# A hybrid decoder layer in split fp32: the sample columns of both FFNs' gate/up moved into the combined products

## The chip, the cores and the metric

The kernel runs on one core of a Trainium2 chip. The metric is the device time of one execution in microseconds; times are medians of several runs on the same chip. One execution was profiled.

## What is computed

One layer for 1024 prompt tokens and 64 sample tokens (8 sequences of 8) that share the weights. `D_MODEL` is 1024, `D_FF` 2816.

```python
def swiglu(x, w_gu, w_down):
    g, u = jnp.split(x @ w_gu, 2, axis=-1)
    return (jax.nn.silu(g) * u) @ w_down

# run_layer, per token group
x = x + 0.5 * rms_norm(swiglu(rms_norm(x, norm_ffn1_pre), ffn1_w_gu, ffn1_w_down), norm_ffn1_post)
h = rms_norm(x, norm_mix_pre)
z = h @ w_in + b_in            # q, k, v of the attention; q, f, i, g of the recurrence
a = rms_norm(windowed_attention(q, k, v, sinks), attn_out_norm)
o = rms_norm(hgrn2(hq, hf, hi), hg_out_norm) * silu(hg)
x = x + rms_norm(concat(a, o) @ w_out, norm_mix_post)
x = x + 0.5 * rms_norm(swiglu(rms_norm(x, norm_ffn2_pre), ffn2_w_gu, ffn2_w_down), norm_ffn2_post)
```

Outputs are the new activations of both groups, the key and value windows and the recurrent states.

## The kernel before

**Split products.** Every large fp32 product is made of three matmuls on rounded halves: an operand is split into `hi` (a copy rounded to fp32r, on ScalarE, line 240) and `lo` (the difference, on VectorE, line 241), and `mm3` (lines 258 to 262) accumulates hi x hi, hi x lo and lo x hi in one PSUM bank. L260, L261 and L262 in the profile are these three. In names, `wsph`/`wspl` are the halves of a weight tile of a head unit, `w` those of a combined product's weights, `h` those of activations, `mm` a PSUM bank.

**Chunks.** The tokens are cut into three chunks: chunk 0 has 256 prompt and the 64 sample tokens (320 columns), chunks 1 and 2 have 384 prompt tokens each.

**Gate/up.** Chunk 0's gate and up are direct products. One head unit `j` (`up0`, line 730; 22 units an FFN) has a g and a u bank, 8 steps of k in each and three matmuls a step, 48 matmuls of 320 columns. `gated0` (line 712) evicts them: in the first FFN both banks are multiplied by `rb` (the root of the pre-norm, lines 718 and 725), Silu runs on ScalarE, and g times u is line 726; in the second FFN the input is normed already and rb is absent. Chunks 1 and 2 are made together by a fast matrix scheme: seven products a unit, 22 units an FFN, each product 4 steps of three matmuls of 384 columns, on seven operands `SF[1..7]` that `pre_x` (first FFN) or `pre_s` with `sums_s` (second) and `factor` prepare. `begin`, `prepare`, `product`, `evict` and `left` make the steps of `up`. In the first FFN `HEAD1 = 9` puts 18 of the 22 chunk-0 units ahead, and the other four are made inside `up` as pieces (`piece`, line 860).

**Order of the work.** The kernel is one stream of program text; a scheduler of the tile framework sets the order of each engine. Beside the large products run "streams": generators that `tick()` (line 102) advances at a given rate, and that `need(name)` runs to their end. `p1` prepares the operands in the first FFN's head. The mixer of each chunk (`m0`, `m1`, `m2`: attention and recurrence) and the norms (`c0`, `c1`, `c2`) run beside the projections and beside the second FFN's head units, which are dealt out by `HEAD2 = (4, 13, 22)`: 4 units, then w_out of chunk 1, then units 4 to 13 beside `m2`, then w_out of chunk 2, then the last 8 beside `c2`. In the mixer, `sc` are attention scores, `pT` the transposed probabilities (TensorE, line 1269, copied by VectorE at 1274), `pv` their product with the values (line 1283).

Weights are loaded by SP's queue; three raw buffers, and `loads0` keeps up to three tiles prepared ahead.

Of the kernel before, what the change touches and what calls it, by code (L numbers as in the profile page):

```python
# [25 lines left out]
WIDTH = [320, 384, 384]  # L26
BLK0 = [0, 2, 5]
# [20 lines left out]
def tile_step(ctx: ExitStack, tc: tile.TileContext, A: dict, O: list):  # L48
# [20 lines left out]
    def hslot(n):  # L69
        w = WIDTH[n]  # L70
        return pp.tile([P, 4, w], F32R, tag=f"h{w}", bufs=8 if w == 384 else 4, name=uid("h"))

    def big(dt=F32, shape=(P, 4, 384)):
        return pp.tile(list(shape), dt, tag="big", bufs=12, name=uid("big"))
# [36 lines left out]

    def need(name):
        st = streams.pop(name, None)
        if st is not None:
            for _ in st[0]:
                pass
# [6 lines left out]
    ones = cp.tile([P, P], F32, name="ones")  # L123
    V.memset(ones, 1.0)
    junk = cp.tile([P, 512], BF16, name="junk")
    omean = cp.tile([P, P], F32, name="omean")
    V.memset(omean, 1.0 / D)
    S.activation(junk[:, :P], ones, AF.Silu)
    cols = cp.tile([P, NROWS], F32, name="cols")
    f1pre = cp.tile([P, KC], F32, name="f1pre")  # L130
    halfpost = cp.tile([P, 16], F32, name="halfpost")
    nsinkb = cp.tile([P, 8], F32, name="nsinkb")
    amask = cp.tile([P, 192], F32, name="amask")
    amask1 = cp.tile([P, P], F32, name="amask1")
    smask = cp.tile([P, 136], F32, name="smask")
    ssink = cp.tile([P, 2], F32, name="ssink")
    seqm = cp.tile([P, 4], F32, name="seqm")
    lmask = {h: cp.tile([P, 32], U8, name=f"lm{h}") for h in LEVELS[2:]}
    ident32 = cp.tile([P, 32], F32, name="ident32")
# [3 lines left out]
    def gains():  # L143
        nc.sync.dma_start(cols, A["cols"])
        V.tensor_scalar(halfpost[:, 0:8], cols[:, C_F1POST:C_F1POST + 8], 0.5, None, op0=ALU.mult)
        V.tensor_scalar(halfpost[:, 8:16], cols[:, C_F2POST:C_F2POST + 8], 0.5, None, op0=ALU.mult)

    def mix_consts():
# [4 lines left out]
        band = tmp2("band", (P, 256))  # L153
        V.memset(band, 0.0)
        G.affine_select(band, band, pattern=[[1, 256]], compare_op=ALU.is_ge, fill=NEG,
                        base=0, channel_multiplier=-1)
        G.affine_select(band, band, pattern=[[-1, 256]], compare_op=ALU.is_ge, fill=NEG,
                        base=P, channel_multiplier=1)
        V.tensor_copy(amask[0:64], band[0:64, 0:192])
        V.tensor_copy(amask[64:P], band[64:P, 64:256])  # L160
        V.tensor_copy(amask1, amask[:, 64:192])
        V.memset(amask1[0:64, 0:64], NEG)
# [5 lines left out]

        s5 = tmp[:, 3, 0:32]
        V.tensor_scalar(s5, row[:, 0:32], 31, None, op0=ALU.bitwise_and)  # L170
        V.tensor_tensor(x[:, 0:32], col[:, 0:32], s5, op=ALU.bitwise_xor)
        V.tensor_copy(tf[:, 1, 0:32], s5)
        V.tensor_copy(tf[:, 1, 32:64], col[:, 0:32])
        V.tensor_tensor(tf[:, 0, 0:32], tf[:, 1, 32:64], tf[:, 1, 0:32], op=ALU.is_gt)
        V.tensor_tensor(ident32, tf[:, 1, 32:64], tf[:, 1, 0:32], op=ALU.is_equal)
        for i, h in enumerate(LEVELS[2:]):
            V.tensor_scalar(tmp[:, 3, 32:64], x[:, 0:32], 4 - i, None, op0=ALU.logical_shift_right)
            V.tensor_copy(tf[:, 1, 64:96], tmp[:, 3, 32:64])
            V.scalar_tensor_tensor(lmask[h], tf[:, 1, 64:96], 1.0, tf[:, 0, 0:32],
                                   op0=ALU.is_equal, op1=ALU.mult)  # L180
# [16 lines left out]
        V.tensor_tensor(smask, tf2[:, 2], tf2[:, 3], op=ALU.add)  # L197

        e = cp.tile([P, 3, 4], F32, name="lbe")
# [34 lines left out]
    def small():  # L234
        return pp.tile([P, 4, 8], F32, tag="small", bufs=10, name=uid("sm"))
# [51 lines left out]
    def tmp2(name, shape=(P, 512)):  # L287
# [1627 lines left out]
```

## Time and profile before

| | |
|---|---|
| median of 3 runs | 1937.2 us (1936.32 to 1937.89) |
| profiled execution: its span, which is its whole time | 1937.4 us |
| TensorE matmuls | 1923.1 us, 13547 |
| VectorE | 1430.7 us, 2469 |
| ScalarE | 946.0 us, 1701 |
| GpSimd | 186.1 us, 227 |
| DMA | 375.56 MB, mean 194 GB/s |

The stages, read from the timeline's changes of matmul shape: first FFN's head 5.65 to 137.8 us; its combined products to 480.5; down and the mixer's first parts to 1106; four head units of the second FFN to 1135; w_out of chunk 1 to 1179.6; ten head units beside `m2` to 1282; w_out of chunk 2 to 1315.2; eight head units beside `c2` to 1374.1; combined products of the second FFN to 1689; down to the end.

A row of the timeline has start, duration, engine, line, operation, output and inputs, shape. A row of the groups has busy time and mean duration behind the first bar and the idle time before them, with what ended it, behind the second. PE is TensorE's matmuls, PEld its weight loads, DVE VectorE, ACT ScalarE, POOL GpSimd, SP SyncE.

### The profile page before, as it was taken

Reading aid. Unit: us, or ns where it says so; the run is one execution under the profiler, and the core shown is the slowest. Engines: PE = TensorE matmul, PEld = TensorE weight load, DVE = VectorE, ACT = ScalarE, POOL = GpSimd, SP = SyncE. Lnnn points to the kernel's source line nnn. Section 1 sums busy time; section 2 is a strip of 40 time slices with the busy share of each in tenths; the row PEclk is TensorE's granted clock in tenths of the full one; section 3 lists DMA queues with packets and bytes.
Section 4 is the critical chain, followed back from the end, with each engine's and each line's share of the span. In section 5 each row is a group of like instructions: output and inputs, shape, how many; then the busy total and the mean of one; then the engine's idle time right before and its main releaser. Section 6 shows DMA issues by size and latency. Waiting matters only on the chain.

```text
span 1937.4 us, 34843 instructions
## 1 busy us (share of the span) xinstructions
PE 1923.1 (99%) x13547; PEld 1806.1 (93%) x13547; DVE 1430.7 (74%) x2469; ACT 946.0 (49%) x1701; POOL 186.1 (10%) x227
## 2 busy tenths in 40 slices
PE   9999999999999999999999999999999999999998
PEld 9999999999998987788999888989999999999886
DVE  6896789877568666787678758756987887656666
ACT  5553444444455434545445545846544444445452
POOL 0300000000004022020221212000000000000102
PEclk9999999999999999999999999999999999999999
DMA  6643676555767556765334344546555555667974
GB/s 248 209 133 115 232 267 247 206 191 184 242 217 242 180 155 215 283 220 163 114 102 153 99 140 142 164 147 209 185 198 192 198 188 189 210 228 241 308 255 141
DMA packets 175750, 375.56 MB, mean 194 GB/s; under 512 B 16144, under 2 KB 67536, under 8 KB 175568
## 3 DMA queue, kind: packets, MB, share of 16 engines
q1 hardware_dynamic: 169680, 362.84, 56.0%
q10 hardware_dynamic: 5904, 10.49, 1.5%
q8 instruction: 106, 1.74, 0.4%
q14 instruction: 60, 0.49, 0.1%
HBM read 290.86 MB, written 83.39 MB: 193 GB/s over the span
## 4 chain that ended last, share of the span: by engine, by line
PE 88%; DMA 6%; DVE 3%; ACT 1%; issue 1%; POOL 1%; SPq 0%; ACTq 0%; DVEq 0%; POOLq 0%
PE mm L260 27%; PE mm L262 26%; PE mm L261 26%; DMA ar<-fa 1%; DMA xt<-in_x_rest_dram 1%; DMA ar<-act 1%; PE lv L1337 1%; PE sc L1237 1%; DMA raw<-in_ffn_w_gu_dram 1%; PE pv L1283 1%; DVE w L241 1%; PE pT L1269 1%; PE c L262 0%; PE c L260 0%; PE c L261 0%
## 5 line engine op out<-in xcount | busy, mean ns | idle before, releaser
L260 PE MATMUL mm<-h,wsph 128*128 128x320 f32 (+1 forms) x1344 | 427.2, 319 | 0.4 <-DVE big L814 0.4
L261 PE MATMUL mm<-h,wsph 128*128 128x320 f32 (+1 forms) x1344 | 425.5, 317 | 0.2 <-DVE h L241 0.2
L262 PE MATMUL mm<-h,wspl 128*128 128x320 f32 (+1 forms) x1344 | 422.6, 316 | 0.0
L241 DVE TENSOR_TENSOR wspl<-raw,wsph 128x1024 fp32r<-128x1024 f32 x208 | 260.8, 1255 | 125.2 <-ACT wsph L240 124.1
L240 ACT CAST wsph<-raw 128x1024 fp32r<-128x1024 f32 x208 | 217.8, 1049 | 254.0 <-PE mm L261 199.3
L260 PEld LDWEIGHTS mm<-h,wsph 128*128 128x128 f32 x1344 | 252.2, 188 | 4.2 <-issue 2.3
L261 PEld LDWEIGHTS mm<-h,wsph 128*128 128x128 f32 x1344 | 252.5, 188 | 3.9 <-issue 2.3
L262 PEld LDWEIGHTS mm<-h,wspl 128*128 128x128 f32 x1344 | 251.9, 188 | 3.4 <-issue 3.1
L240 ACT CAST w<-raw 128x512 fp32r<-128x512 f32 (+1 forms) x208 | 153.8, 745 | 199.9 <-PE mm L261 96.2
L261 PE MATMUL mm<-h,w 128*128 128x384 f32 (+1 forms) x736 | 245.6, 334 | 0.3 <-DVE h L622 0.3
L260 PE MATMUL mm<-h,w 128*128 128x384 f32 (+1 forms) x736 | 245.7, 334 | 0.2 <-ACT h L620 0.2
L262 PE MATMUL mm<-h,w 128*128 128x384 f32 (+1 forms) x736 | 239.6, 333 | 0.5 <-POOL w L613 0.4
L241 DVE TENSOR_TENSOR w<-raw,w 128x512 fp32r<-128x512 f32 (+1 forms) x208 | 178.3, 861 | 72.6 <-ACT w L240 71.7
L261 PE MATMUL mm<-w,h 128*128 128x512 f32 x462 | 180.5, 391 | 0.7 <-DVE w L241 0.7
L260 PE MATMUL mm<-w,h 128*128 128x512 f32 x462 | 180.8, 394 | 0.0
L262 PE MATMUL mm<-w,h 128*128 128x512 f32 x462 | 179.8, 391 | 0.0
L260 PE MATMUL mm<-big,w 128*128 128x384 f32 x528 | 176.7, 335 | 0.3 <-ACT big L806 0.2
L261 PE MATMUL mm<-big,w 128*128 128x384 f32 x528 | 176.5, 334 | 0.0
L262 PE MATMUL mm<-big,w 128*128 128x384 f32 x528 | 176.0, 334 | 0.0
L261 PEld LDWEIGHTS mm<-h,w 128*128 128x128 f32 x736 | 138.1, 188 | 1.1 <-DVE h L622 0.8
L260 PEld LDWEIGHTS mm<-h,w 128*128 128x128 f32 x736 | 138.1, 188 | 0.8 <-ACT h L620 0.5
L262 PEld LDWEIGHTS mm<-h,w 128*128 128x128 f32 x736 | 137.6, 188 | 1.0 <-POOL w L613 0.7
(367 smaller groups left out, 3353.8 us busy)
## 6 DMA issues: line engine op xcount, KB each, us to landing
raw<-in_ffn_w_gu_dram SPq DMA_DIRECT2D x162, 512.0 KB
raw<-in_ffn_w_down_dram SPq DMA_DIRECT2D x74, 512.0 KB
raw<-in_w_in_dram SPq DMA_DIRECT2D x54, 512.0 KB
ar<-fa SPq DMA_DIRECT2D x70, 384.0 KB
big<-in_ffn_w_down_dram SPq DMA_DIRECT2D x88, 256.0 KB
fb<-big SPq DMA_DIRECT2D x44, 512.0 KB
fa<-big SPq DMA_DIRECT2D x22, 768.0 KB
raw<-fb SPq DMA_DIRECT2D x30, 512.0 KB
```

The costliest lines, as they stand in the source:

```text
L240: made['S'] = S.copy(hi, src).ins
L241: (lo_eng or V).tensor_tensor(lo, src, hi.bitcast(F32), op=ALU.subtract)
L260: PE.matmul(out, a[0], b[0], start=first, stop=False, skip_group_check=resume)
L261: PE.matmul(out, a[0], b[1], start=False, stop=False, skip_group_check=resume)
L262: return PE.matmul(out, a[1], b[0], start=False, stop=last, skip_group_check=resume).ins
L1237: PE.matmul(banks[g][rows(hq), i, cs], zq[rows(g), 2 * pr + i, b * P + 64 * hq:b * P + 64 * hq + 64], kx[rows(g), k0 + cs.start:k0 + cs.st ...
L1269: PE.transpose(tb2[hq][:, g, i, slot], pt[g][rows(hq), c:c + P], ident[rows(hq), rows(hq)])
L1283: PE.matmul(ob[par][rows(g), :, hq], vn[rows(par), b + (blk + hq) // 2, rows(g)], pT[hq][rows(par), g, :, PLACE[hq][blk]], start=alone or ...
L1337: PE.matmul(b5[32 * i:32 * i + 32, b, a], K[:, a, cs], Q[:, a, cs], start=True, stop=True)
```

## The change

The 64 sample columns leave chunk 0's gate/up, which now has 256 columns (`WU`). Of them 32 (`XT`) are appended to each of the two 384-column chunks, so that the combined products have 416 columns (`WS`); the host lays out the inputs accordingly, in the second FFN a DRAM tile `extra` carries the columns over, and `evict` stores the sample columns of its result to `acts` (a store more in each combined unit).

First FFN: all 22 chunk-0 units run in the head (`HEAD1 = NK`), and the pieces in `up` go. The factor rb on u goes; it is applied at the eviction of the down product, from a DRAM copy `rootd`, as a VectorE product (256 columns) and a ScalarE copy (64).

Second FFN: `hi` and `lo` of chunk 0 lie side by side in `hh` tiles; a step is one 512-column matmul (w_hi with hi and lo) and one 256-column matmul (w_lo with hi), and the halves of a bank are added in the eviction (`S.copy`, then `V.tensor_tensor`). `HEAD2` becomes (3, 11, 22), `c2` gets a rate of its own (1.1), and `need("p1")` and `need("c2")` ahead of the combined products give way to `f.feed`, which advances the stream when an operand is missing.

Further: factor 5's low half goes from VectorE to GpSimd; the `wf`, `t2` and `small` buffers become 3, 7 and 5 (from 4, 8 and 10); mask constants are rebuilt in the mixer or kept in DRAM; the attention's output gain is applied after the transposes on ScalarE and VectorE; the sample gather has 8 DMAs for 16.

```diff
+WU, XT = 256, 32
+WS = 384 + XT
...
     def factor(SF, m, src):
         new = (lambda: hslot(1)) if m in (1, 2, 4, 5) else (lambda: big(F32R))
-        hi, lo = SF[m] = new(), new()
+        hi, lo = new(), new()
         S.copy(hi, src)
         yield
-        V.tensor_tensor(lo, src, hi.bitcast(F32), op=ALU.subtract)
+        (G if m in (5,) else V).tensor_tensor(lo, src, hi.bitcast(F32), op=ALU.subtract)
+        SF[m] = hi, lo
...
         def gated0(j, g, rb):
-            w = WIDTH[0]
+            w = WU
             t = tmp2("sg")
-            if rb is None:
-                S.copy(t[:, :w], g[:, :w])
-            else:
-                V.tensor_tensor(t[:, :w], g[:, :w], rb, op=ALU.mult)
+            V.tensor_tensor(t[:, :w], g[:, :w], rb, op=ALU.mult)
             S.activation(t[:, :w], t[:, :w], AF.Silu)
             def rest(u):
-                v = u
-                if rb is not None:
-                    v = tmp2("su")
-                    V.tensor_tensor(v[:, :w], u[:, :w], rb, op=ALU.mult)
-                V.tensor_tensor(t[:, :w], t[:, :w], v[:, :w], op=ALU.mult)
-                return nc.sync.dma_start(acts[:, j], t[:, :w]).ins
+                V.tensor_tensor(t[:, :w], t[:, :w], u[:, :w], op=ALU.mult)
+                return nc.sync.dma_start(acts[:, j, :w], t[:, :w]).ins
...
         def product(u, m):
+            while m not in f.SF:
+                next(f.feed)
...
-            bk = chains[u, c][:, :384]
+            bk = chains[u, c][:, :WS]
...
             elif m == 3:
                 V.tensor_tensor(e[:, 1], bk, e[:, 1], op=ALU.add)
                 act(0)
+                nc.sync.dma_start(acts[:, j, WU:].rearrange("p (h t) -> p h t", h=2), e[:, 0:3:2, 384:])
...
                         if kp == NK - 1:
-                            S.copy(y[hf][:, i, :w], bank[:, :w])
+                            if tag == 1:
+                                V.tensor_tensor(y[hf][:, i, :WU], bank[:, :WU], rt, op=ALU.mult)
+                                S.copy(y[hf][:, i, WU:w], bank[:, WU:w])
+                            else:
+                                S.copy(y[hf][:, i, :w], bank[:, :w])
...
         def head(js):
             wts = loads0(js)
             for j in js:
-                up0(j, wts)
+                banks = mmbank(), mmbank()
+                t = tmp2("sg")[:, :WU]
+                for bank in banks:
+                    wt = wts.next()
+                    for k in range(KC):
+                        hl = h[0][k // 2][:, k % 2]
+                        PE.matmul(bank, wt[0][:, k], hl.rearrange("p l t -> p (l t)"), start=k == 0, stop=False,
+                                  skip_group_check=True)
+                        PE.matmul(bank[:, :WU], wt[1][:, k], hl[:, 0], start=False, stop=k == KC - 1,
+                                  skip_group_check=True)
+                        if k % 4 == 3:
+                            tick()
+                    v = tmp2("sv")[:, :WU]
+                    S.copy(v, bank[:, WU:])
+                    if bank is banks[0]:
+                        V.tensor_tensor(t, bank[:, :WU], v, op=ALU.add)
+                        S.activation(t, t, AF.Silu)
+                    else:
+                        V.tensor_tensor(v, bank[:, :WU], v, op=ALU.add)
+                        V.tensor_tensor(t, t, v, op=ALU.mult)
+                nc.sync.dma_start(acts[:, j, :WU], t)
...
-    HEAD1, HEAD2 = 9, (4, 13, 22)
+    RA0, RA1, RB0, RB1, RB2 = 1.2, 0.75, 0.6, 0.8, 1.1
+    HEAD1, HEAD2 = NK, (3, 11, 22)
...
-        f2.begin(units(NK))
-        need("c2")
+        f2.begin(UNITS)
+        f2.feed = feed("c2")
```

The order of three places changes as follows. TensorE beside the mixer of chunk 2, before: the last transposes `pT` of a block are followed by a transpose `kT` and then by 26 matmuls of head units (the first are shown) ahead of the block's `pv`.

```order
L1269 MATMUL pT_13230<-ident,t_1888_13116 128x64
L1269 MATMUL pT_13231<-ident,t_1888_13116 128x64
L1269 MATMUL pT_13230<-ident,t_1888_13116 128x64
L1269 MATMUL pT_13231<-ident,t_1888_13116 128x64
L1446 MATMUL kT_13252<-ident,big_10934 128x128
L260 MATMUL mm_13371<-h_11489,wsph_13167 128x320
L261 MATMUL mm_13371<-h_11491,wsph_13167 128x320
L262 MATMUL mm_13371<-h_11489,wspl_13168 128x320
L260 MATMUL mm_13372<-h_11488,wsph_13214 128x320
```

After, at the same block: the head unit's steps are pairs of 512 and 256 columns (`hh` is the side-by-side operand), and `pv` follows the transposes with nothing between.

```order
L1054 MATMUL mm_13317<-hh_11548,wsph_13170 128x512
L1056 MATMUL mm_13317<-hh_11548,wspl_13171 128x256
L1293 MATMUL pT_13182<-ident,t_1892_13079 128x64
L1293 MATMUL pT_13183<-ident,t_1892_13079 128x64 x2
L1293 MATMUL pT_13183<-ident,t_1891_13074 128x64 x2
L1293 MATMUL pT_13182<-ident,t_1892_13079 128x64
L1293 MATMUL pT_13182<-ident,t_1891_13074 128x64 x2
L1293 MATMUL pT_13182<-ident,t_1892_13079 128x64
L1293 MATMUL pT_13183<-ident,t_1892_13079 128x64
L1293 MATMUL pT_13182<-ident,t_1892_13079 128x64
L1293 MATMUL pT_13183<-ident,t_1892_13079 128x64
L1307 MATMUL pv_13221<-t_1909_13200,vn_10610 64x2x64
```

The matmuls that stood between have moved ahead of the transposes or behind the block.

VectorE at the start of the first FFN's head, before: after `rb`, one weight subtraction, and then both banks of the first units are evicted in turn (`sg` from a g bank, `su` from a u bank).

```order
L305 SCALAR_TENSOR_TENSOR rb_316<-mq_327,rt_318 128x320
L241 TENSOR_TENSOR wspl_384<-raw_381,wsph_383 128x1024
L718 TENSOR_TENSOR sg_399<-mm_147,rb_316 128x320
L725 TENSOR_TENSOR su_402<-mm_148,rb_316 128x320
L718 TENSOR_TENSOR sg_406<-mm_149,rb_316 128x320
L725 TENSOR_TENSOR su_409<-mm_150,rb_316 128x320
L718 TENSOR_TENSOR sg_413<-ax_151,rb_316 128x320
```

After:

```order
L289 SCALAR_TENSOR_TENSOR rb_307<-mq_318,rt_309 128x256
L225 TENSOR_TENSOR wspl_376<-raw_373,wsph_375 128x1024
L710 TENSOR_TENSOR sg_391<-mm_138,rb_307 128x256
L710 TENSOR_TENSOR sg_396<-mm_140,rb_307 128x256
L710 TENSOR_TENSOR sg_401<-ax_142,rb_307 128x256
L225 TENSOR_TENSOR wspl_382<-raw_379,wsph_381 128x1024
L149 TENSOR_SCALAR nsinkb<-nsinkb 128x8
L294 SCALAR_TENSOR_TENSOR ss_433<-ss_433,sq_435 128x416
L225 TENSOR_TENSOR wspl_388<-raw_385,wsph_387 128x1024
L714 TENSOR_TENSOR sg_391<-sg_391,mm_139 128x256
```

The g banks are evicted first, and the first u bank (`mm_139`) behind two more weight subtractions and a sum of squares.

VectorE beside the last head units of the second FFN, before: the wide operations of `c2` stand in one group between two weight subtractions.

```order
L241 TENSOR_TENSOR wspl_14856<-raw_14853,wsph_14855 128x1024
L471 TENSOR_TENSOR h_14923<-big_14846,h_14922 128x1536
L534 TENSOR_TENSOR big_13575<-big_13575,big_14847 128x1536
L471 TENSOR_TENSOR h_15009<-big_14746,h_15008 128x1536
L471 TENSOR_TENSOR big_14885<-big_14847,big_14884 128x1536
L241 TENSOR_TENSOR wspl_14893<-raw_14890,wsph_14892 128x1024
```

After:

```order
L225 TENSOR_TENSOR wspl_14674<-raw_14671,wsph_14673 128x1024
L1063 TENSOR_TENSOR sg_14640<-mm_14638,sv_14667 128x256
L521 TENSOR_TENSOR big_14552<-big_14551,big_13264 128x1664
L523 TENSOR_TENSOR big_14403<-big_13264,big_14403 128x1664
L225 TENSOR_TENSOR wspl_14708<-raw_14705,wsph_14707 128x1024
L1066 TENSOR_TENSOR sv_14697<-mm_14639,sv_14697 128x256
L525 TENSOR_TENSOR big_13502<-big_13502,big_14552 128x1664
L460 TENSOR_TENSOR h_14656<-big_14473,h_14655 128x1664
L225 TENSOR_TENSOR wspl_14734<-raw_14731,wsph_14733 128x1024
```

They are wider, and at most two stand between two weight subtractions.

302 lines of the change are left out of this document (157 added, 145 removed).

## The prediction

> **What bounds the kernel now.** I read the page first, then the rate of TensorE in single stages, then the stages in which the change moves work. The page:
>
> ```profile
> span 1937.4 us, 34843 instructions
> PE 1923.1 (99%) x13547; PEld 1806.1 (93%) x13547; DVE 1430.7 (74%) x2469; ACT 946.0 (49%) x1701; POOL 186.1 (10%) x227
> PEclk9999999999999999999999999999999999999999
> PE 88%; DMA 6%; DVE 3%; ACT 1%; issue 1%; POOL 1%; SPq 0%; ACTq 0%; DVEq 0%; POOLq 0%
> ```
>
> TensorE is busy 99% of the span at the full clock, and the chain that ended last is 88% matmuls. So the kernel ends when the matmuls are through, and the change is first a sum over matmuls. The span, 1937.4 us, is the profiled execution's whole time, 0.2 us from the median of the runs, 1937.2; I work with 1937.4. The three runs lie within 1.6 us, and about 0.2% (3.9 us) is what can be told from no change: faster is below 1933.3, slower above 1941.1.
>
> A matmul's duration overlaps its successor's, so its price is the distance of starts. In the timeline, nine starts lie between the first and the last row at 384 and at 320 columns, six at 512 (one row in three is shown, and all have one line of the three in turn):
>
> ```profile
> 1450.06 0.33 PE L260 MATMUL mm<-big,w 128*128 128x384 f32 x1
> ...
> 1451.62 0.33 PE L260 MATMUL mm<-big,w 128*128 128x384 f32 x1
> 1352.08 0.31 PE L260 MATMUL mm<-h,wsph 128*128 128x320 f32 x1
> ...
> 1353.40 0.31 PE L260 MATMUL mm<-h,wsph 128*128 128x320 f32 x1
> 1805.02 0.39 PE L260 MATMUL mm<-w,h 128*128 128x512 f32 x1
> ...
> 1806.38 0.39 PE L260 MATMUL mm<-w,h 128*128 128x512 f32 x1
> 828.23 1.47 PE L457 MATMUL tr<-ident,big 128*128 128x128 f32 x12
> L457 PE MATMUL tr<-ident,big x48: 270/272/328, 822.2 to 903.0; 128*128 128x128 f32 x48
> ```
>
> 1.56/9 = 173.3 ns, 1.32/9 = 146.7 and 1.36/6 = 226.7. These three lie on one line, 13.3 ns + 0.4167 ns a column. It gives 120.0 ns for 256 columns and 186.7 for 416, which this trace does not show. The last two rows bound 256 from below: twelve transposes of 128 columns, each with a weight tile of its own, take (1.47 - 0.27)/11 = 109 ns each, where the line would give 66.6. So a weight load costs about 109 ns, and 256 columns may cost 109 to 146.7 (the 320 price); I take 120, above the load.
>
> **The matmuls.** Counts by shape:
>
> ```profile
> L260 PE MATMUL mm<-h,wsph 128*128 128x320 f32 x1056 | 328.1, 311 | 0.4 <-DVE big L814 0.4
> L260 PE MATMUL mm<-h,w 128*128 128x384 f32 x704 | 235.4, 334 | 0.0
> L260 PE MATMUL mm<-big,w 128*128 128x384 f32 x528 | 176.7, 335 | 0.3 <-ACT big L806 0.2
> ```
>
> Each of the three lines of a product has as many, so the combined products are 3 x (704 + 528) = 3696 matmuls at 384 columns, and chunk 0's gate/up is 22 units x 48 = 1056 matmuls of 320 in each FFN (in the first, 192 of them as pieces among the combined products).
> First FFN, chunk 0: 1056 x (120.0 - 146.7) = -28.2 us. Second: 1056 x 146.7 = 154.9 becomes 352 x (226.7 + 120.0) = 122.0, so -32.9. Combined products: 3696 x 13.3 = +49.3. Net -11.8 us, that is 1925.6 if everything else stays hidden.
> The Trainium skill ("TensorE: Matmul & The Clock Gate", Back-to-back issue gap) states columns/2.4 + 2.5 ns: the slope agrees, the fixed part here is 13.3. By its figures the sum would be -28.1 - 29.0 + 49.3 = -7.8, since fewer, wider matmuls save less where the fixed part is small; the measured line decides.
>
> **What the matmuls hide.** Shorter head units ask more of VectorE. Its rows, and the windows of the second FFN's head stage (whole; beside mixer chunk 2; w_out of chunk 2; beside the norm stream of chunk 2), of the first FFN's head and of a stretch of combined products (columns: window, length, then busy of PE, PEld, DVE, ACT, POOL, with counts):
>
> ```profile
> L241 DVE TENSOR_TENSOR wspl<-raw,wsph 128x1024 fp32r<-128x1024 f32 x208 | 260.8, 1255 | 125.2 <-ACT wsph L240 124.1
> L726 DVE TENSOR_TENSOR sg<-sg,mm x22: 474/483/490, 1114.5 to 1374.8; 128x320 f32<-128x320 f32 x22
> L471 DVE TENSOR_TENSOR h<-big,h 128x1536 fp32r<-128x1536 f32 x8 | 14.0, 1751 | 0.1
> L1293 DVE TENSOR_TENSOR t<-pv,t x14: 410/418/426, 810.8 to 1277.0; 128x256 f32<-128x256 f32 x14
> 1179.60:1374.10 194.50, 193.77 (x1498) 182.17 (x1497) 137.09 (x277) 125.90 (x249) 7.57 (x21) 1.00 0.51 164
> 1179.60:1282.00 102.40, 101.67 (x941) 95.83 (x940) 74.71 (x192) 73.35 (x164) 7.57 (x21) 1.00 0.48 154
> 1282.00:1315.20 33.20, 33.20 (x151) 27.49 (x150) 15.04 (x20) 14.73 (x25) 0.00 (x0) 1.00 0.50 156
> 1315.20:1374.10 58.90, 58.90 (x410) 58.86 (x409) 47.34 (x66) 37.82 (x62) 0.00 (x0) 1.00 0.55 185
> 70.00:140.00 70.00, 70.00 (x474) 69.73 (x474) 66.58 (x83) 36.97 (x49) 8.98 (x6) 1.00 0.49 152
> 1500.00:1600.00 100.00, 100.00 (x579) 100.00 (x578) 80.07 (x139) 42.91 (x84) 0.00 (x0) 1.00 0.54 197
> ```
>
> *Second FFN's head.* A unit's TensorE time falls from 48 x 0.1467 = 7.04 to 16 x 0.3467 = 5.55 us; VectorE's rises from 2 x 1.255 + 0.483 = 2.99 to 2 x 1.255 + 3 x 0.418 = 3.76. The stage now holds 19 units instead of 18: TensorE 194.5 - 126.7 + 105.4 = 173.2, VectorE 137.1 - 53.8 + 71.4 = 154.7, or 89% where it was 70%. The row of 70 to 140 us shows 95% with TensorE never idle, so this can hold; but the mixer's chains have fewer matmuls to hide behind:
>
> ```profile
> 1253.28 0.35 DVE L1247 CUSTOM_DVE_ANT_0 t<-sc,amask 128x192 f32<-128x192 f32 x1
> 1258.38 0.19 ACT L1259 ACTIVATE sm<-sm 128x4 f32<-128x4 f32 x1
> 1272.22 0.59 PE L1269 MATMUL pT<-ident,t 64*128 64x64 f32 x12
> 1272.74 0.42 PE L261 MATMUL mm<-h,wsph 128*128 128x320 f32 x1
> 1272.99 0.31 PE L262 MATMUL mm<-h,wspl 128*128 128x320 f32 x1
> 1273.66 0.89 PE L1283 MATMUL pv<-t,vn 64*64 64x128 f32 x24 [0.36 <-DVE t L1274]
> ```
>
> From the end of pT (1272.22 + 0.59) to pv are 0.85 us through VectorE's copy. After the change pv directly follows pT in places where 26 head matmuls stood between. Three such places cost 3 x 0.85 = 2.6. The softmax from sc to pT takes over 5.1 us (first to second row); where only 16 half-width steps (8 x 0.3467 = 2.8 us) cover it, some 1 to 2.6 stays open: I take one such, 1.0. Sum +3.6, with 0 (the trace's other idle places shrink as well) and 12 (all of it open at each of the last blocks) as bounds.
>
> *Chunk 2's norm stream* beside the last head units: VectorE has 47.3 of 58.9 us now. Its eight 1536-wide operations become 1664 wide (L471 is one, 1.75 us, so 1.90), and in the new order pairs of them stand between two weight subtractions: 2 x 1.90 + 1.255 = 5.05 us against a bank's 2.77, twice, then 1.90 + 1.255 + 0.42 = 3.57 against 2.77, three times: 7.0 short. Prepared ahead are one bank (2.8) or two (5.5). Before, four such operations, 7.0 us, stand between two subtractions there, and TensorE is busy 58.90 of 58.90 us; that speaks for two, and I take 7.0 - 5.5 = +1.5 (0 to 7).
>
> *w_out of chunk 2* closes with its operand's split uncovered by head matmuls: +0.5 (0 to 1).
>
> *First FFN.* The rb products on u go, but the u bank's only eviction now comes after the Silu, so the banks of the first three units come free later. Rows at that place:
>
> ```profile
> 26.84 1.22 DVE L241 TENSOR_TENSOR wspl<-raw,wsph 128x1024 fp32r<-128x1024 f32 x1
> 27.98 0.48 DVE L718 TENSOR_TENSOR sg<-mm,rb 128x320 f32<-128x320 f32 x1
> 28.38 0.48 DVE L725 TENSOR_TENSOR su<-mm,rb 128x320 f32<-128x320 f32 x1
> 46.30 0.56 DVE L310 SCALAR_TENSOR_TENSOR ss<-ss,sq 128x384 f32<-128x384 f32 x1 [2.12 <-ACT sq L321]
> ```
>
> A weight subtraction takes 1.14 start to start, a 256-wide product about 0.34 (0.40 x 256/320, a little over). In the new order the first freed u bank stands behind three weight subtractions, three such products and a sum of squares: 3 x 1.14 + 3 x 0.34 + 0.6 + its own 0.34 = 5.4 us, while the first g bank opens at 1.5 and lasts 24 x 0.12 = 2.9: the u bank waits 1.0. Later, VectorE has 6.70 us a unit (66.58/70 x 7.04); it becomes 2.51 + 0.84 + (6.70 - 2.51 - 1.45) x 1.083 = 6.3 against 5.76, so 0.56 short over the 12 units that the stream p1 spans, 6.7, less the two banks prepared ahead, 5.8: another 1.0. Together +2.0 (0 to 6).
>
> *At nothing:* the combined products' evictions grow by 8%, under TensorE's own 8% (VectorE 80% there, last window). Each unit's new store of sample columns waits on SP for a VectorE product, with the next weight load queued behind it:
>
> ```profile
> SPq L826 <- DVE big L825: 55.5, 9, 7.1
> L1585 POOL TENSOR_TENSOR big<-big,big 128x1024 f32<-128x1024 f32 x4 | 10.0, 2511 | 32.0 <-PE sav L1582 32.0
> 49.21 1.31 DVE L726 TENSOR_TENSOR sg<-sg,su 128x320 f32<-128x320 f32 x1
> 47.03 9.52 POOL L311 TENSOR_TENSOR ss<-ss,sq 128x384 f32<-128x384 f32 x6 [34.14 <-DVE ss L310]
> ```
>
> Stores there already hold SP up to 7.1 us with TensorE full; a unit lasts 84 x 0.187 = 15.7 us, so a load still comes in time; without that cover each unit would lose up to the 7.1. The down eviction with rt, the eight sample gathers for sixteen, the rebuilt masks and the smaller pools lie beside matmuls, 0 (-1 to +1).
>
> Sum: -11.8 + 3.6 + 1.5 + 0.5 + 2.0 = -4.2, or **1933.2 us**.
>
> **Rivals.**
> *A: the covers hold*, as VectorE's 95% in the first FFN suggests: 1925.6. Against it: the 95% has no mixer chain beside it.
> *B: VectorE paces the second FFN's head.* Its queue is in order, and weight subtractions wait behind the mixer's operations. At 81% of VectorE the stage lasts 154.7/0.81 = 191, 17.8 more than 173.2: with the first FFN's 2.0, 1925.6 + 17.8 + 2.0 = 1945.4, slower. At 85% it is 1936.4, no change. It turns slower where the share stays under 83% (1941.1 - 1925.6 - 2.0 = 13.5 above 173.2). For it: the stage now shows 70%, 73% beside the mixer. Against it: VectorE was not asked for more there.
> *C: a 256-column matmul costs what 320 do*, bound by its weight load: 1408 x 26.7 = +37.6, so 1971.3. Against it: 109 ns a load.
> *D: GpSimd blocks VectorE.* Factor 5's low half moves to GpSimd in both heads, 2.51 x 1664/1024 = 4.1 us long. The last two rows show L726 at 1.31 us beside a GpSimd addition, 0.48 alone. If VectorE stands still for 4.1 us and saves its own 1.9, each FFN loses 2.2: 1933.2 + 4.4 = 1937.6.
> The Trainium skill ("SBUF — State Buffer", Who interferes with whom) says so: a VectorE instruction with two SBUF inputs contends with a GpSimd instruction that reads SBUF, and the loser blocks fully; L726 agrees.
>
> **Chances.** Forecast 0.43 (its own range 1929 to 1938; 0.20 of it faster), A 0.26, B 0.21 (0.16 slower), C 0.05, D 0.05. Faster 0.20 + 0.26 = 0.46; slower 0.16 + 0.05 = 0.21; same 0.33. The range reaches from just under A to the middle of B, 1925 to 1944.5; C and the worst of B stay out.
>
> **What would show it.** Starts 120 ns apart at 256 columns and 187 at 416; the second FFN's head stage near 173 us plus 5, with TensorE idle before pv and before pT behind VectorE; one idle of 1 us near 32 us at the first u bank. Wrong if head matmuls wait mostly for wspl throughout (B), if 256 columns cost 145 ns (C), or if the stage shows no idle (A).

## The result and the profile after

The changed kernel takes 1983.41 us (median of 4, 1981.5 to 1985.56), the kernel before on the same chip 1937.55. The ratio is 1.0233, with a 95% interval of 1.0219 to 1.0248: 2.3% slower, where 0.2% faster was forecast. Of the runs reported below, one of e9 took 6451 us and stands outside e9's median and ratio. The profiled execution of the changed kernel took 1980.5 us, 43.1 more than that of before. Its page:

```profile
span 1980.5 us, 34547 instructions
PE 1943.8 (98%) x13195; PEld 1787.7 (90%) x13195; DVE 1464.1 (74%) x2518; ACT 975.9 (49%) x1763; POOL 203.0 (10%) x230
PE 83%; DVE 6%; DMA 5%; ACT 2%; issue 2%; POOL 1%; SPq 1%; DVEq 0%; ACTq 0%; POOLq 0%
```

TensorE idles 36.7 us now (14.3 before), and its busy time rose by 20.7 us although the sum over matmuls had come to -11.8. The chain of the last work has twice the share of VectorE and five points less of TensorE. Where this lies is read from windows cut where the matmuls change shape (first head; combined products and down; pairs, mixer and projections; second head's stage with both w_out; combined products and down; pairs to the end). Before:

```profile
1.15:137.79 136.64, 135.54 (x899) 133.13 (x899) 116.29 (x164) 75.80 (x111) 19.61 (x14) 1.00 0.61 203
137.79:565.35 427.56, 426.77 (x2566) 425.55 (x2565) 323.43 (x567) 194.86 (x349) 2.43 (x6) 1.00 0.60 210
565.35:1106.60 541.25, 537.90 (x4517) 473.34 (x4515) 396.01 (x758) 264.58 (x509) 119.62 (x150) 1.00 0.56 176
1106.60:1374.08 267.48, 266.75 (x2501) 246.04 (x2501) 183.46 (x349) 159.59 (x309) 20.50 (x32) 1.00 0.48 155
1374.08:1772.45 398.37, 398.26 (x2379) 397.75 (x2377) 300.23 (x487) 177.81 (x318) 0.00 (x0) 1.00 0.60 207
1772.45:1937.40 164.95, 157.85 (x697) 130.26 (x695) 111.05 (x145) 73.34 (x108) 23.42 (x20) 0.99 0.70 233
```

After (columns as in the prediction: window, length, busy time of PE, PEld, DVE, ACT, POOL, then the granted clock):

```profile
1.15:147.49 146.34, 137.94 (x1086) 134.48 (x1087) 122.91 (x165) 84.98 (x123) 29.48 (x15) 0.99 0.64 220
147.49:576.31 428.82, 427.67 (x2378) 423.03 (x2377) 320.50 (x526) 192.95 (x340) 1.54 (x7) 1.00 0.62 210
576.31:1121.87 545.56, 544.51 (x4514) 474.88 (x4513) 399.40 (x796) 271.79 (x531) 120.38 (x146) 1.00 0.53 177
1121.87:1383.74 261.87, 243.98 (x2151) 201.82 (x2151) 196.79 (x396) 167.03 (x343) 26.58 (x37) 0.98 0.47 154
1383.74:1811.12 427.38, 427.36 (x2379) 423.14 (x2377) 313.41 (x491) 185.81 (x321) 0.00 (x0) 1.00 0.58 195
1811.12:1980.50 169.38, 162.32 (x697) 130.37 (x695) 110.86 (x145) 73.34 (x108) 24.54 (x20) 0.99 0.68 228
```

Against the sum over matmuls, stage by stage:

| stage | before | by the matmul sum | after | over |
|---|---|---|---|---|
| first head | 136.6 | 136.6 (22 x 5.76 for 18 x 7.04) | 146.3 | 9.7 |
| combined and down, first FFN | 427.6 | 424.0 (-4 x 7.04 + 1848 x 0.0133) | 428.8 | 4.8 |
| pairs, mixer, projections | 541.3 | 541.3 | 545.6 | 4.3 |
| second head's stage | 267.5 | 234.6 (-154.9 + 122.0) | 261.9 | 27.3 |
| combined and down, second FFN | 398.4 | 423.0 | 427.4 | 4.4 |
| pairs to the end | 165.0 | 165.0 | 169.4 | 4.4 |

The four small excesses, 17.9 us together, stand in stages in which TensorE, taken together, idles no longer than before (9.3 us for 11.4), two of them without any edit to their matmuls. Of the other two, 37.0 us, 24.5 are additional idle time (7.3 and 17.2) and the rest is longer busy time, with the granted clock at 0.99 and 0.98 where it was 1.00. The timeline tells the first kind; first and last row of six starts at 512 columns in the last stage, of six at 416 in the combined products, and of nine at 256 in the first head:

```profile
1899.81 0.39 PE L244 MATMUL mm<-w,h 128*128 128x512 f32 x1
...
1901.21 0.39 PE L244 MATMUL mm<-w,h 128*128 128x512 f32 x1
1400.07 0.35 PE L244 MATMUL mm<-big,w 128*128 128x416 f32 x1
...
1401.20 0.35 PE L244 MATMUL mm<-big,w 128*128 128x416 f32 x1
90.06 0.28 PE L245 MATMUL mm<-h,wsph 128*128 128x256 f32 x1
...
91.14 0.28 PE L245 MATMUL mm<-h,wsph 128*128 128x256 f32 x1
```

Six starts at 512 columns take 1.40 us, 233.3 ns each, in code that was not touched (226.7 before). Six at 416 take 1.13, 188.3 (189.0 over all 3690 pairs of them), where the line gave 186.7. Nine at 256 take 1.08, 120.0, as forecast. What TensorE waits for in the second head's stage (engine and line, released by, total, times, longest):

```profile
PE pv L1307 <- DVE t L1298: 5.8, 4, 3.1
PE mm L1054 <- DVE sv L1066: 3.8, 2, 2.7
PE mm L1054 <- DVE sg L1063: 2.8, 2, 2.0
PE mm L244 <- ACT h L1230: 1.1, 1, 1.1
```

pv behind the copy of pT, as the prediction had it, and head matmuls behind the two additions that free their banks (L1063, L1066), which it had not. The longest wait for pv starts at 1270.32, where the last transpose ends. VectorE stood idle at that moment, for 3.3 us in all:

```profile
1270.70 1.23 DVE L225 TENSOR_TENSOR wspl<-raw,wsph 128x1024 fp32r<-128x1024 f32 x1 [3.29 <-ACT wsph L224]
1272.71 0.68 DVE L1298 COPY t<-pT 128x512 f32<-128x512 f32 x1
1273.44 1.56 PE L1307 MATMUL pv<-t,vn 64*64 64x128 f32 x24 [3.12 <-DVE t L1298]
```

It waited for ScalarE to round a weight tile; the copy of pT stood behind that tile's subtraction and two operations of the mixer, and so began 2.4 us after its input was there.

### The profile page after: what moved, and what is told of

Its sections match the earlier page's. It is cut to its first block, busy times and chain, and to the rows that moved or that the text cites. A ratio compares the mean times of both kernels' runs of the same rounds, so it can differ in the third digit from the quotient of the medians.

```text
span 1980.5 us, 34547 instructions
## 1 busy us (share of the span) xinstructions
PE 1943.8 (98%) x13195; PEld 1787.7 (90%) x13195; DVE 1464.1 (74%) x2518; ACT 975.9 (49%) x1763; POOL 203.0 (10%) x230
## 4 chain that ended last, share of the span: by engine, by line
PE 83%; DVE 6%; DMA 5%; ACT 2%; issue 2%; POOL 1%; SPq 1%; DVEq 0%; ACTq 0%; POOLq 0%
PE mm L244 24%; PE mm L246 24%; PE mm L245 24%; PE mm L1054 3%; DMA big<-in_ffn_w_down_dram 2%; PE mm L1056 2%; DMA raw<-in_ffn_w_gu_dram 2%; DVE w L225 1%; DVE wspl L225 1%; PE lv L1361 1%; DVE t L748 1%; DMA ar<-act 1%; PE sc L1261 1%; PE pv L1307 1%; ACT wsph L224 1%
## 5 line engine op out<-in xcount | busy, mean ns | idle before, releaser
L225 DVE TENSOR_TENSOR wspl<-raw,wsph 128x1024 fp32r<-128x1024 f32 x216 | 269.0, 1246 | 119.6 <-ACT wsph L224 109.1
L224 ACT CAST wsph<-raw 128x1024 fp32r<-128x1024 f32 x216 | 226.0, 1048 | 234.5 <-PE mm L245 138.8
L244 PE MATMUL mm<-h,wsph 128*128 128x320 f32 (+2 forms) x1056 | 329.1, 314 | 3.9 <-DVE sg L710 2.6
L245 PE MATMUL mm<-h,wsph 128*128 128x320 f32 (+2 forms) x1056 | 328.9, 312 | 0.2 <-DVE h L1231 0.2
L246 PE MATMUL mm<-h,wspl 128*128 128x320 f32 (+2 forms) x1056 | 327.2, 311 | 0.8 <-DVE wspl L225 0.6
L246 PE MATMUL mm<-h,w 128*128 128x416 f32 (+1 forms) x736 | 257.3, 350 | 0.7 <-POOL w L607 0.5
L244 PE MATMUL mm<-h,w 128*128 128x416 f32 (+1 forms) x736 | 256.4, 348 | 0.8 <-ACT big L798 0.5
L245 PE MATMUL mm<-h,w 128*128 128x416 f32 (+1 forms) x736 | 254.9, 346 | 0.5 <-DVE h L616 0.3
L244 PEld LDWEIGHTS mm<-h,wsph 128*128 128x128 f32 x1056 | 199.2, 189 | 8.7 <-issue 4.3
L245 PEld LDWEIGHTS mm<-h,wsph 128*128 128x128 f32 x1056 | 199.9, 189 | 4.3 <-issue 3.5
L246 PEld LDWEIGHTS mm<-h,wspl 128*128 128x128 f32 x1056 | 199.7, 189 | 3.1 <-DVE wspl L225 1.7
L246 PE MATMUL mm<-big,w 128*128 128x416 f32 x528 | 186.3, 353 | 0.2 <-DVE w L225 0.2
L244 PE MATMUL mm<-big,w 128*128 128x416 f32 x528 | 185.5, 351 | 0.0
L245 PE MATMUL mm<-big,w 128*128 128x416 f32 x528 | 184.6, 350 | 0.0
L224 ACT CAST w<-t 128x512 fp32r<-128x512 f32 x176 | 108.1, 619 | 95.2 <-PE mm L246 91.7
L245 PEld LDWEIGHTS mm<-h,w 128*128 128x128 f32 x736 | 138.3, 188 | 2.9 <-DVE h L616 0.9
L244 PEld LDWEIGHTS mm<-h,w 128*128 128x128 f32 x736 | 138.2, 188 | 2.7 <-ACT big L798 0.9
```

The costliest lines, as they stand in the source:

```text
L224: made['S'] = S.copy(hi, src).ins
L225: (lo_eng or V).tensor_tensor(lo, src, hi.bitcast(F32), op=ALU.subtract)
L244: PE.matmul(out, a[0], b[0], start=first, stop=False, skip_group_check=resume)
L245: PE.matmul(out, a[0], b[1], start=False, stop=False, skip_group_check=resume)
L246: return PE.matmul(out, a[1], b[0], start=False, stop=last, skip_group_check=resume).ins
```

## The experiments

All are variants of the changed kernel unless they say before. Each was timed against the kernel before on its chip (1937.2 to 1938.2).

**Where tiles start.** e1 and e2 put one more 32-byte tile ahead of all others:

```diff
+    shift = cp.tile([P, 8], F32, name="shift")
+    V.memset(shift, 0.0)
     mhalf = cp.tile([P, 8], F32, name="mhalf")
```

> The changed kernel with one unused 32-byte tile put first, so that every SBUF tile lies 32 bytes further. In the changed kernel the 512-column matmuls of the unchanged down stages start 233.2 ns apart (226.7 before) and the 416-column ones 189.0 (the line gives 186.7): together about 23 us. Theory P (it is where the tiles lie: all start at a multiple of 64 bytes now, 32 past one before): 512 columns return to 226.7, 416 to 186.7, and the time falls by about 20 to 23 us to 1960 to 1964. Rival R (it goes with the width of the new tiles, their stride of 1664 bytes, or with the heat of the chip): the time stays at 1980 to 1985.

> The kernel before with the same 32-byte tile put first, so that its tiles start at multiples of 64 bytes as in the changed kernel. Theory P: its 512-column matmuls go from 226.7 to about 233 ns (1866 of them, +12 us), its 384-column ones from 173.3 to about 175 (4560, +8 us), the 320-column ones stay: about 1957. Rival R: 1937, no change.

e1: 1984.59 us (ratio 1.0242, 1.0225 to 1.0259). e2: 1937.41 (0.9998, 0.9988 to 1.0007). Theory P falls: the common start of the tiles is not it, from either side.

**How wide the tiles are.** The change made the activation tiles 416 columns wide, 1664 bytes a row of k for 1536. e4 keeps the tiles and packs 384 columns at the old stride wherever 384 or 320 columns are used:

```diff
+    def packed(t):
+        return t if t.shape[-1] != WS else t.rearrange("p k w -> p (k w)")[:, :4 * 384].rearrange("p (k w) -> p k w", k=4)
...
-        return [[hslot(n), hslot(n)], [hslot(n), hslot(n)]]
+        return [[packed(hslot(n)) for _ in range(2)] for _ in range(2)]
...
-                t = hslot(1).rearrange("p (k l) w -> p k l w", k=2)[:, :, :, :384]
+                t = packed(hslot(1)).rearrange("p (k l) w -> p k l w", k=2)
```

> The changed kernel, in which activations of 384 and 320 columns are packed at a stride of 384 (1536 bytes) inside their 416-wide tiles, in the projections and in both down stages; the combined products keep the stride of 1664 bytes. Theory Q (a matmul slows down where its moving operand and the weights that are loaded meanwhile lie differently within 256 bytes; 1664 is 6.5 x 256, 1536 is 6 x 256): 512 columns return from 233.2 to 226.7 ns (1866 of them, -12 us), 384 from 175 to 173.3 (-1.5), the 416s stay: about 1969 to 1972. Rival H (the wide matmuls run slower because the chip does, whatever the layout): no change, 1980 to 1985.

e5 does the reverse to the kernel before, and has one temporary buffer fewer (`t2`, 7 for 8) to make room:

```diff
-        return pp.tile([P, 4, w], F32R, tag=f"h{w}", bufs=8 if w == 384 else 4, name=uid("h"))
+        return pp.tile([P, 4, 400 if w == 384 else w], F32R, tag=f"h{w}", bufs=8 if w == 384 else 4, name=uid("h"))[:, :, :w]
```

> The kernel before with its 384-column activation tiles allocated 400 wide (stride 1600 bytes, 6.25 x 256), and one temporary buffer less to make room; the work is the same. Theory Q: its 512-column matmuls go from 226.7 towards 233 and the 384-column ones that read these tiles from 173.3 to 175 to 177, together +10 to +20 us, 1947 to 1957. Rival H: 1937, no change.

e4: 1976.91 us (1.0201, 1.0184 to 1.0218), 6.5 less than the changed kernel. e5: 1951.33 (1.0071, 1.0056 to 1.0086), 14 more than before. The buffer is not the cause: TensorE's busy time rose by 14.2 us (1937.3 for 1923.1) and its idle time fell (11.6 for 14.3), so what was lost lies in longer matmuls. The 512-column matmuls of the last stage, six starts, in e4 and then in e5:

```profile
1899.74 0.39 PE L247 MATMUL mm<-w,h 128*128 128x512 f32 x1
...
1901.10 0.39 PE L247 MATMUL mm<-w,h 128*128 128x512 f32 x1
```

```profile
1870.11 0.40 PE L260 MATMUL mm<-w,h 128*128 128x512 f32 x1
...
1871.49 0.39 PE L260 MATMUL mm<-w,h 128*128 128x512 f32 x1
```

1.36/6 = 226.7 ns again in e4, 1.38/6 = 230 in e5, where it had been 226.7. In these matmuls the activations are the stationary operand, in the combined products the moving one. Rival H falls, and Theory Q stands as far as the row stride goes; that it is the place within 256 bytes is not shown. The combined products keep their stride in e4 and their price, 189.0 ns. That the stride is at work there too is argued from the changed kernel's trace: each step of k lies 1664 bytes, 6.5 x 256, further, and the spacing alternates with it; the three matmuls of a step start 187.5 ns apart in about half of the steps and 190.5 in the others. The gain of e4 fell short of its range: the two stages with pairs came out 3.1 and 4.5 us shorter, where 12 had been counted for all 512s, and the first head 3.0 us longer, with the clock at 0.97 for 0.99. Its windows of the first head and of the last stage:

```profile
1.15:150.48 149.33, 140.43 (x1087) 137.34 (x1087) 123.22 (x165) 84.87 (x123) 29.99 (x15) 0.97 0.65 216
1810.06:1974.90 164.84, 157.84 (x697) 130.27 (x695) 111.04 (x145) 73.43 (x108) 24.55 (x20) 0.99 0.70 234
```

The last stage is back at 164.8 us.

**GpSimd and VectorE.** e3 moves factor 5's low half back:

```diff
-        (G if m in (5,) else V).tensor_tensor(lo, src, hi.bitcast(F32), op=ALU.subtract)
+        V.tensor_tensor(lo, src, hi.bitcast(F32), op=ALU.subtract)
```

> The changed kernel with factor 5's low half back on VectorE, nothing else. In the changed kernel a 4-column VectorE operation lasted 3.76 us and a 1664-wide one 5.49 us beside GpSimd's 6.84 us subtraction, and TensorE idled 3.6 us behind the first and 3.4 us behind the second. Theory D (GpSimd blocks VectorE there): both go, VectorE gets 1.9 us more work twice, 2 to 7 us faster. Rival B alone (VectorE is full there whoever does the subtraction): no change or up to 4 us slower.

1982.06 us (1.0227, 1.0211 to 1.0242): no change that can be told. The contention is real, as VectorE's and GpSimd's rows of the changed kernel, and VectorE's of e3, show:

```profile
102.62 3.76 DVE L186 TENSOR_TENSOR lbe<-cols,lbe 128x4 f32<-128x4 f32 x1
99.52 6.84 POOL L460 TENSOR_TENSOR h<-big,h 128x1664 fp32r<-128x1664 f32 x1 [25.13 <-ACT h L458]
```

```profile
104.12 0.16 DVE L186 TENSOR_TENSOR lbe<-cols,lbe 128x4 f32<-128x4 f32 x1
```

A 4-column operation takes 3.76 us beside GpSimd's subtraction and 0.16 without. The Trainium skill ("SBUF — State Buffer", Who interferes with whom) has this as a lock that stops the loser for the whole of an instruction; the rows agree. In e3 TensorE's wait of 1.4 us behind it is gone, but after another wait (see the next experiment) the clock stayed at half for 6.8 us where it had been 3.4, and the first head ends at 147.2 us for 147.5. So the medians show no price of the contention at this place, and the two traces do not settle what it would be at an equal clock.

**The first head.** e10 sets the rate of p1:

```diff
-P1 = 1.0
+P1 = 0.7
```

> The changed kernel with P1 = 0.7 for 1.0, so that the operands of the combined products are prepared over 71 of the first head's 76 ticks instead of 50. The first head ends at 147.5 us, 9.3 later than before, with VectorE busy without a break from 98 to 117 us and half idle after 120. Theory F (VectorE is short while p1 runs): the head ends 4 to 8 us earlier, 1976 to 1979. Rival G (the first unit's banks and the rb chain hold TensorE): no change, within 2 us.

1978.07 us (1.0210, 1.0193 to 1.0227); the head ends at 143.25 us, 4.2 earlier, in Theory F's range. But what went is not what it names. The longest wait of the changed kernel's first head is TensorE's for the last of six sums of squares that p1 has on GpSimd:

```profile
PE rb L279 <- POOL ss L295: 2.6, 1, 2.6
```

In e10 this wait is gone, and so is the drop of the clock that came during it (1.00 over the head for 0.99). The waits for VectorE's evictions and weight subtractions are not shorter: 4.6 us in e10, 4.1 in the changed kernel. With the wait for GpSimd, the 4.1 us and the clock, which is worth some 1.5 us (an estimate: half of 3.4 us, less a part in which TensorE idled), about 8 of the 9.7 us are accounted for.

**The second head's stage.** e6 gives the mixer of chunk 2 two more head units; e7 has the plain head; e8 and e9 take work from VectorE; e11 slows that mixer:

```diff
-    HEAD1, HEAD2 = NK, (3, 11, 22)
+    HEAD1, HEAD2 = NK, (1, 11, 22)        # e6; (1, 12, 22) in e11
...
-    RM = [0.88, 1.08, 1.24]
+    RM = [0.88, 1.08, 0.98]               # e11
```

The plain head of e7, with which e12 is built too:

```diff
-                        PE.matmul(bank, wt[0][:, k], hl.rearrange("p l t -> p (l t)"), ...)
-                        PE.matmul(bank[:, :WU], wt[1][:, k], hl[:, 0], ...)
+                        mm3(bank[:, :WU], (wt[0][:, k], wt[1][:, k]), (hl[:, 0], hl[:, 1]), k == 0, k == KC - 1)
...
-                    v = tmp2("sv")[:, :WU]
-                    S.copy(v, bank[:, WU:])
                     if bank is banks[0]:
-                        V.tensor_tensor(t, bank[:, :WU], v, op=ALU.add)
-                        S.activation(t, t, AF.Silu)
+                        S.activation(t, bank[:, :WU], AF.Silu)
                     else:
-                        V.tensor_tensor(v, bank[:, :WU], v, op=ALU.add)
-                        V.tensor_tensor(t, t, v, op=ALU.mult)
+                        V.tensor_tensor(t, t, bank[:, :WU], op=ALU.mult)
```

e8 has this eviction under the wide matmuls, and so leaves out the right half of each bank; in e9 the loads make high halves only (`return hi, hi`).

> The changed kernel with two head units moved from ahead of w_out of chunk 1 into the stage beside chunk 2's mixer (HEAD2 = 1, 11, 22: ten units there for eight). That stage shows about 14 us of idle TensorE in 95 us. Theory B2 (too few head matmuls to cover the mixer's chains of waits): two units more cover 5 to 10 us of it, 1973 to 1979. Rival B1 (VectorE is short of time in the whole stage): the idle time moves with the units, 1980 to 1986.

> The changed kernel with the second FFN's head in three 256-column matmuls a step instead of a 512- and a 256-column one; Silu reads the g bank and one product the u bank, so a unit costs VectorE 0.84 us and ScalarE two copies less, TensorE 5.76 us for 5.55 (+0.21 x 22 = +4.6). Theory B1 (VectorE's evictions pace the stage): the stage's idle time of about 20 us falls by more than 4.6, 1965 to 1980. Rival B2 (chains of the mixer): idle time falls only by the longer matmuls, no change to +4, 1981 to 1988.

> The changed kernel, whose second head's eviction leaves out the right half of each bank (the product of the weights' high and the activations' low part): Silu reads the g bank and one product the u bank, so VectorE has 0.84 us and ScalarE two copies less a unit, while the matmuls stay 512 and 256. The first to last head stage of the second FFN takes 261.8 us in the changed kernel, about 27 more than its matmuls need. Theory B1 (VectorE and ScalarE pace the stage): 8 to 18 us faster, 1965 to 1975. Rival B2 (the mixer's chains are too long for the cover): 0 to 4 us faster.

> The changed kernel, whose second head leaves out the low halves of its weights (the 256-column matmul reads the high half again): VectorE has 2.51 us a unit less, ScalarE and the matmuls stay. Theory B1: the stage loses nearly all of its idle time, 15 to 27 us faster, 1956 to 1968. Rival B2: 0 to 5 us faster.

> The changed kernel with chunk 2's mixer at 0.98 steps a tick for 1.24, and HEAD2 = (1, 12, 22), so that twelve units stand beside it for nine. A tick is 4 steps of k: 1.76 us of matmuls before, 1.39 after the change, so 1.24 steps a tick became 0.89 steps/us from 0.70; 0.98 gives 0.70 again. Theory T (the mixer is dealt out too fast for its chains of waits, so TensorE reaches a chain's next matmul before its operand): the stage from first to last head unit falls from 261.8 by 8 to 18 us, 1965 to 1975. Rival B1 (VectorE's share as such): the stage stays within 4 us, 1979 to 1986.

The part beside the mixer needs 32.2 us for the mixer's own matmuls (102.64 - 10 x 7.04 before) and 5.55 us a unit, 5.76 with the plain head. The column behind it is the whole stage's length over what its matmuls need (234.6; 239.3 plain), the last one TensorE's idle time in the whole stage and the granted clock:

| kernel | us, ratio (interval) | units | beside the mixer: length, over need | whole stage, over need | idle, clock |
|---|---|---|---|---|---|
| changed | 1983.4, 1.0233 (1.0219 to 1.0248) | 9 | 99.2, 17.0 | 27.3 | 17.9, 0.98 |
| e6 more units | 1984.2, 1.0240 (1.0225 to 1.0255) | 11 | 113.8, 20.5 | 28.4 | 17.2, 0.97 |
| e7 plain head | 1979.6, 1.0217 (1.0202 to 1.0233) | 9 | 93.6, 9.6 | 20.0 | 12.8, 0.98 |
| e8 no additions | 1979.1, 1.0214 (1.0199 to 1.0229) | 9 | 95.5, 13.3 | 25.8 | 13.2, 0.95 |
| e9 no low halves | 1975.4, 1.0190 (1.0173 to 1.0207) | 9 | 93.9, 11.7 | 18.4 | 10.2, 0.99 |
| e11 slower mixer | 1991.9, 1.0280 (1.0263 to 1.0297) | 12 | 110.2, 11.4 | 29.8 | 17.4, 0.97 |

So neither more cover (e6) nor VectorE's load as such explains all of it: e9 takes 2.5 us a unit from VectorE and still leaves 18.4 of 27.3, with 10.2 of 17.9 us of idle time. e8 took 4.7 us of idle time away, but in its profiled run, the longest of its four, the clock was lower (0.95 for 0.98) and TensorE's busy time 3.2 us longer, so that only 1.5 us of the stage was gained. A slower mixer lowered the excess beside it but was not through by w_out of chunk 2, where TensorE then waited 5.6 us. The whole stage became 2.5 us longer, and the combined products behind it 6.5 (433.9 us for 427.4), with a wait of 3.6 us for a rounded weight tile at their start. e6 and e7 came out in B1's range, e8 just beyond B2's, e9 and e11 in none: each theory saw a part.

Two of them together did more. e12 has the packed tiles, P1 = 0.7, the plain head and the slower mixer with twelve units; e13 is e12 with the wide head, e14 is e13 with the additions left out.

> The changed kernel with the packed activations (-6.5 measured alone), P1 = 0.7 (-5.3), the plain second head (-3.8) and the slower mixer of chunk 2. If they add up without the last: 1967.8. Theory T adds 8 to 15 to that: 1953 to 1960, still above the kernel before (1937). Rival: the plain head and the slower mixer remove the same idle time, 1963 to 1968.

> The kernel of e12 (packed activations, P1 = 0.7, twelve units beside a slower mixer) with the second head's matmuls of 512 and 256 columns as in the change. With the plain head its stage beside the mixer is 102.5 us long and needs 101.3. Theory E (the wide form's eviction holds the banks: a ScalarE copy and a VectorE addition in two queues before a bank is free): the stage is again 8 to 12 us longer than the 98.8 that its matmuls need, total 1974 to 1982. Rival T (the mixer's rate alone was too high): it needs 98.8 and takes 99 to 102, total 1958 to 1964.

> The kernel of e13, with the right half of each bank left out at the eviction (the product of the weights' high and the activations' low part), so that a bank is freed by one ScalarE or VectorE operation as in the plain head, with the matmuls of the wide one. Theory E: the stage beside the mixer comes to 99 to 102 us, total 1957 to 1963. Rival T: the same as e13 within 3 us.

e12: 1964.75 us (1.0140, 1.0125 to 1.0155). e13: 1976.55 (1.0201, 1.0183 to 1.0219). e14: 1967.61 (1.0152, 1.0134 to 1.0171). The part beside the mixer of e12, e13 and e14:

```profile
1170.27:1272.80 102.53, 101.00 (x1013) 95.01 (x1010) 82.06 (x200) 73.58 (x159) 10.91 (x24) 1.00 0.51 169
```

```profile
1165.40:1276.17 110.77, 103.94 (x931) 87.23 (x930) 86.69 (x220) 80.67 (x182) 11.65 (x24) 0.97 0.49 159
```

```profile
1170.02:1273.45 103.43, 100.58 (x914) 85.38 (x913) 79.99 (x197) 72.58 (x151) 11.80 (x24) 0.98 0.52 167
```

Over their need they are 1.2, 12.0 and 4.6 us. Only the head's form differs between the kernels of e12 and e13, and only the eviction between e13 and e14. The stretches hold 437, 547 and 530 matmuls of the mixer; the difference is mostly 96 of 32 columns in e13 and e14, which take about 1 us. The clock's share is larger: 0.97 over e13's stretch is worth up to 3.3 us, 0.98 over e14's 2.1 (length times what is missing), and e12 has lost nothing to it. In e13 TensorE waits for the additions again (total, times, longest):

```profile
PE mm L1057 <- DVE sv L1069: 4.4, 3, 3.3
...
PE mm L1057 <- DVE sg L1066: 2.3, 2, 2.0
```

e12 came out in its rival's range: the plain head and the slower mixer remove partly the same idle time, yet beside the mixer hardly any is left. Theory E holds there: with the mixer slow enough, the wide head's eviction costs 7.3 of the 10.8 us, the clock drops behind its waits included, though VectorE is busy only 78% of the time in e13. That it is not the work but the place is argued, not shown: the bank is free only after a copy at ScalarE's turn and an addition at VectorE's, each behind the mixer's operations, but e14 also takes 6.7 us of VectorE and 8.1 us of ScalarE away. For the place speak the 78% and the wait for pv above, ahead of which VectorE stood idle. e13's total came out in Theory E's range with the help of its combined products, which took 433.9 us for 426.9 in e12. The total of e14 came out above its range, since its mixer ended late and w_out of chunk 2 waited 4.5 us.

## Why the prediction was wrong

**The price of matmuls that nobody edited.** The sum took every other matmul as unchanged, and 416 columns from the line at 186.7 ns. Both failed: 189.0 for 416 columns (3696 x 2.3 = 8.5 us) and 233.3 for most 512s, together the 17.9 us of the four stages. e4 and e5 show the cause for the 512s, the tile stride of 1664 bytes; for the 416s it is argued, since no run packs them. This stood under no rival.

**The cover in the second head's stage.** Forecast were +5.6 us, measured 27.3. By the terms of the sum: beside the mixer 17.0 for +3.6 (0 to 12), w_out of chunk 2 3.2 for +0.5 (36.4 us for 33.2), beside the norm stream 5.9 for +1.5 (64.0 us where 58.9 - 8 x 7.04 + 10 x 5.55 = 58.1 are needed):

```profile
1283.38:1319.77 36.39, 35.12 (x149) 27.24 (x150) 16.44 (x29) 17.60 (x35) 0.00 (x0) 1.00 0.50 160
1319.77:1383.74 63.97, 60.94 (x346) 53.03 (x345) 59.04 (x87) 44.02 (x76) 5.16 (x1) 0.97 0.56 191
```

The step that failed is the reading of the window of 70 to 140 us, with which rival B was set aside: 95% of VectorE with TensorE full was read as room for 89% beside the mixer. The stretch that was priced at 173.2 us of matmuls took 199.5 (1184.22 to 1383.74) with VectorE busy for 151.3 us of it, 76%, so even B's own price, 191 at 81%, was too small. And B's mechanism was only in part the right one: the runs put the idle time down to turns on two engines, of the mixer's chains and of the evictions, and not to the sum of VectorE's work alone. The evictions were costed as 3 x 0.42 us of VectorE, never as time for which a bank is held; e13 and e14 show what that costs with the slower mixer, 7.3 us. In the changed kernel itself, e8 takes 4.7 of 17.9 us of idle time away with them.

**The clock** stood in no term. Before, it was granted in full up to the last microseconds; the changed kernel's waits brought three drops to half, of 13.7 us together. The mean clock, 0.996 for 0.999, makes that some 6 us of the 43 (an estimate: 0.003 of the span).

**pv behind pT** was right in kind and small in size: 5.8 us in four places for 2.6 in three. One place lasted 3.1 us, and the clock dropped during it.

**The first head**: +2.0 forecast, 9.7 measured. The idle at the first u bank near 32 us, forecast at 1.0, did not come. VectorE's shortage while p1 runs, forecast at 1.0, is the 4.1 us of waits for its evictions and weight subtractions. The wait of 2.6 us for GpSimd's sum of squares stood in no term; it is what e10 removes, together with the clock drop.

**Right**: 256 columns at 120.0 ns (rival C out; its sum comes to 1970.8, not 1971.3), and the combined products' evictions and SP's stores at nothing, with TensorE busy 427.36 of 427.38 us. Rival D's contention is there, with a GpSimd subtraction of 6.84 us where 4.1 was reckoned, but e3 finds no price of it. Rival A fails with the covers.

What stays open: nearly 2 us of the first head, what in the layout sets the price of a stride, and in the second head's stage how the mixer's chains share the remainder with the evictions. e12 still has about 14 us over its need there, 7.4 of them idle: its last head unit stands behind the first two matmuls of the combined products and ends at 1371.9 us. No version of the change tried here beats the kernel before.

## What to carry to other kernels

A change of a tile's width is a change of stride for every matmul that reads it, the untouched ones too. The strides that cost here, 1664 and 1600 bytes, are no multiples of 256, and those that did not, 1536 and 1280, are; four strides make no rule, so measure the new stride, or keep the old one. Where matmuls hide other engines' chains, a saving on matmuls is not worth its sum: count how long each PSUM bank or operand waits for its turn on other engines, not how busy they are, and add what such a wait costs in clock. A utilisation that one stage sustains says nothing of a stage with dependent chains.

## What the runs showed of the hardware

A stride of 1664 or 1600 bytes for 1536 cost up to 6.6 ns on a 512-column matmul and about 2 on 384 columns, nothing on average on 320 (146.6 ns in either kernel). At 416 columns, which were run at 1664 bytes alone, a matmul took 2.3 ns more than the line gives.

The clock dropped after short idle times. Around the wait of 3.1 us for pv at 1270.3, in steps of 2 us (the granted clock is the third number from the right):

```profile
1268.00:1270.00 2.00, 2.00 (x22) 1.61 (x22) 0.00 (x0) 2.00 (x10) 0.00 (x0) 1.00 0.10 40
1270.00:1272.00 2.00, 0.32 (x12) 0.18 (x6) 1.30 (x2) 2.00 (x4) 0.29 (x2) 1.00 0.00 0
1272.00:1274.00 2.00, 0.56 (x12) 0.56 (x16) 2.00 (x4) 1.14 (x3) 0.29 (x2) 0.52 0.33 97
1274.00:1276.00 2.00, 2.00 (x36) 1.52 (x28) 1.71 (x4) 0.37 (x1) 0.00 (x0) 0.50 0.48 182
1276.00:1278.00 2.00, 2.00 (x9) 1.59 (x6) 1.49 (x10) 0.04 (x1) 0.00 (x0) 0.50 0.80 275
1278.00:1280.00 2.00, 2.00 (x11) 1.68 (x10) 0.09 (x2) 1.92 (x9) 0.00 (x0) 0.78 0.10 35
```

It was half from 1272.1 us on (0.52 over the third row), 1.8 us into the wait, for 6.8 us, so a stall of 3 us can cost up to twice itself (an estimate: 6.8 us at half the clock are 3.4 us of matmuls). The Trainium skill ("TensorE: Matmul & The Clock Gate", The HAM clock gate) gives about 3.4 us of idle time for the gate to close and as much busy time to open. Here less sufficed: 1.8 us of this wait, 2.2 of the wait of 2.6 in the first head, and at 1371.1 us the wait of 2.0 for L1063, after which the clock was half for 3.4 us.
